# Weight differences fetched, used and stored in another order, and the output projection's transposes in two halves

## The chip, the cores and the metric

The kernel runs on one core of a Trainium2 chip. Its engines work side by side, each through its own queue of instructions in order: TensorE (PE; its weight loads are shown as PEld), VectorE (DVE), ScalarE (ACT), GpSimd (POOL) and SyncE (SP). SP and POOL issue nearly all transfers (DMA). The metric is the device time of one execution in microseconds, as the median of several runs.

## The reference

One layer of a hybrid encoder, for a prompt of 2048 rows (16 tiles of 128) and eight short samples (one more tile, called SAMPLE). All is float32, the model width is 1024.

```python
h   = rms_norm(x, norm_g[0])
z   = h @ w_in                                   # split into heads
att = rms_norm(band_attention(qa, ka, va, rel), g_att)
hb  = mlstm(qb, kb, vb, ib, fb); hb = headnorm(hb) * g_mlstm * sigmoid(ob)
mix = concat([att, hb], axis=-1) @ w_out         # the output projection
x   = x + rms_norm(mix, norm_g[1])
u   = conv3(rms_norm(x, norm_g[2]) @ w_up) + b_conv     # 2 x 2816 columns
x   = x + rms_norm((gelu(u_gate) * u_up) @ w_down, norm_g[3])
```

## The kernel before, in words

A float32 product is made from three products of a rounded form: each operand is split into a high part (a cast on ACT) and a low part (a difference on DVE), and `mm3` (L109 to L113) multiplies high by high, high by low and low by high. So every operand costs ACT one cast and DVE one difference before TensorE can use it: for the weights in `split` (L1352 to L1354), for turned rows in `rows_to_T` (L218 and L219).

The work has three stages. The input projection takes w_in group by group, with the attention and the recurrent memory (mlstm) run beside it in two pipelines. The output projection, `project`, goes over the tiles 0 to 7, SAMPLE, 8 to 15. Then the feed-forward network takes the tiles in three blocks of six, six and five.

The feed-forward products use a scheme of fast matrix multiplication: the operands are cut into 2 x 2 blocks and seven products of sums of blocks stand for eight. For the down-projection the sums of weight blocks are needed: from the blocks B11, B12, B22, B21 of each of the NK = 11 parts of w_down (called 0, 1, 2, 3 in the code), the generator `folds` makes T1 = B12 - B11 (in place of 0), T3 = B22 - B12 (in place of 1), T2 = T1 - B22 (in place of 2) and T4 = B21 + T2 (in place of 3), and stores them in DRAM (`wtd`), from where the down-projection fetches them some hundred microseconds later. A block is 128 x 512, 256 KB. Fetches and stores (`load`, L1210, and `store`, L1217) are issued by POOL; the four operations of a part (`make`, L1213) run on DVE. The three kinds are kept in program order on their engines. The blocks lie in a pool of six buffers, `spare`: a fetch into a buffer waits until the store from it has landed.

`folds` is a generator that is pulled along by `project`: a counter `owed` grows by FOLD_RATE after each half of each sum (68 points in all: 17 tiles, two sums, two halves), and for each whole unit one step of `folds` is traced. What is left at the end is traced after the last tile. So a step is a place in program order; a planner, which works with its own estimate of times, then lays out each engine's queue.

For a tile, `project` does this: the rows `mr` (fetched by SP, two buffers) are normed (ACT square sum L1021, POOL L94 and L100, DVE scale L1023); `turn_rows` transposes them in eight blocks of 128 x 128 on TensorE (L83, into `mT_pt`) and splits them into `mt` (L218, L219); two sums `wo` of 512 columns and 24 products each follow; DVE (L1057) and ACT (L1059) read each sum; POOL makes the factor `n_rs`, DVE adds the residual (L1069), SP stores the row to `x2d` (L1070). The turn of the next tile is traced between the two sums of the present one. The accumulators in PSUM are two of 512 columns (`ps_mm`, tag "mm"), which hold the sums, and two of 1024 columns (`ps_big`, tag "big"), which the attention uses for its scores (`s`) and their transposes (`pt`). Tiles 0 to 7 turn in two halves through `ps_mm`; SAMPLE and tiles 8 to 15 turn in one piece through `ps_big`, with one cast and one difference of 1024 columns.

While tile 7 is worked on the two pipelines are drained, and from tile 8 on the first pieces of the feed-forward input (`h2_units`, transposes `h2T_pt`, through other accumulators) are made beside the projection. After the last tile its weights' memory is given back, the first weights of the up-projection (`wu`, `wuh`, `wul`) are split, and four kept pieces `lated` are fetched and split (`late_B`, L1197 to L1199).

Of the kernel before, what the change touches and what calls it, by code (L numbers as in the profile page):

```python
# [38 lines left out]
HALF = [384, 384, 320]  # L39
PAIRS = [[(((b[j], 0), (b[j + 3], 0)), j * P, P, f"{b[j]}") for j in range(3)] for b in FBLOCKS[:2]]  # L40
NK = NF // 2
FOLD_RATE = 1.0
FAST = (0, 1, 2)
ORDERS = [[f for k in range(NK) for f in (k, k + NK)] if b in FAST else list(range(NF)) for b in range(3)]
B11, B12, B22, B21 = range(4)
# [5 lines left out]
def hymba_step(ctx: ExitStack, tc: tile.TileContext, I: dict, O: dict):  # L51
# [12 lines left out]
    def ps_big(name):  # L64
        return psum.tile([P, 1024], F32, tag="big", name=name)
# [10 lines left out]
    def spare_tile(name):  # L76
        return spare.tile([P, 512], F32, tag="k", name=name)
# [4 lines left out]
    def transpose(out, in_, n=P):  # L82
        nc.tensor.transpose(out, in_, ident[:n, :n])  # L83
# [125 lines left out]
    def rows_to_T(hrow, chunk, j, name, bank):  # L209
        w = 4 if bank is not ps_big else KT  # L210
        for q in range(KT // w):
            pt = bank(f"{name}_pt{q}")
            for k in range(w):
                transpose(pt[:, k * P:(k + 1) * P], hrow[:, (w * q + k) * P:(w * q + k + 1) * P])
            ptv = pt.rearrange("p (k t) -> p k t", k=w)
            hv = chunk[:, 0, w * q:w * q + w, j * P:(j + 1) * P]
            lv = chunk[:, 1, w * q:w * q + w, j * P:(j + 1) * P]
            nc.scalar.copy(hv, ptv)  # L218
            nc.vector.tensor_tensor(lv, ptv, hv, op=ALU.subtract)  # L219
# [733 lines left out]

    wo = []
    g1 = []
    gatt = const.tile([P, 4], F32, name="gatt")

    def w_out_steps():
# [39 lines left out]
    def project(tiles):  # L998
# [25 lines left out]
            s.mt = mt[:, :2 * D].rearrange("p (a k n) -> p a k n", a=2, k=KT)  # L1024

        def turn_rows(s):
            rows_to_T(s.m, s.mt, 0, f"mT{s.t}", ps_mm if s.t < 8 else ps_big)

        fold, owed = folds(), [0.0]
        load(ss[0])  # L1030
        norm(ss[0])
        yield 0.0, 0.3
        turn_rows(ss[0])
        load(ss[1])
        yield 0.9, 1.2
        for n_, s in enumerate(ss):
# [7 lines left out]
            for hf in range(2):  # L1044
                c = slice(hf * 512, hf * 512 + 512)
                acc = ps_mm(f"wo{t}_{hf}")
                for k in range(KT):
                    mm3(acc, s.mt[:, 0, k, :], s.mt[:, 1, k, :], wo[k][0][:, c], wo[k][1][:, c],
                        start=(k == 0), stop=(k == KT - 1))
                    if k % 4 == 3:  # L1050
                        owed[0] += FOLD_RATE
                        while owed[0] >= 1:
                            owed[0] -= 1
                            next(fold, None)
                        yield 2.6, 0.5
                ssq = small.tile([P, 1], F32, tag="wssq", name=f"wssq{t}_{hf}")
                nc.vector.tensor_tensor(m[:, c], acc, g1[0][:, c], op=ALU.mult)  # L1057
                idle = m[:, 512:D] if hf == 0 else s.mt[:, 0, 0:4, :].rearrange("p k n -> p (k n)")
                nc.scalar.activation(idle, acc, AF.Square, accum_out=ssq)  # L1059
                if hf == 0:  # L1060
                    ssa = ssq
                    mean_square(ssa, ssq, D)
                    if nxt:
                        turn_rows(nxt)
                        if n_ + 2 < len(ss):
                            load(ss[n_ + 2])
                        yield 0.9, 1.2
# [133 lines left out]
    def folds():  # L1201

        keep = tc.keep_in_program_order
        sub, plus = ALU.subtract, ALU.add
        live = {}

        def load(k, xs):
            for x in xs:
                live[k, x] = spare_tile(f"fold{k}_{x}")
                keep(nc.gpsimd.dma_start(live[k, x], I["w_down"][k][:, x * 512:(x + 1) * 512]))  # L1210

        def make(k, o, x, y, op):
            keep(nc.vector.tensor_tensor(live[k, o], live[k, x], live[k, y], op=op))  # L1213

        def store(k, xs):
            for x in xs:
                keep(nc.gpsimd.dma_start(wtd[k][:, x * 512:(x + 1) * 512], live.pop((k, x))))  # L1217

        for k in range(NK + 1):
            now, old = k < NK, k > 0  # L1220
            if old:
                make(k - 1, 2, 0, 2, sub)
            if now:
                load(k, (0, 1))
            yield
            if old:
                store(k - 1, (0, 1))
                make(k - 1, 3, 3, 2, plus)
            yield
            if old:  # L1230
                store(k - 1, (2, 3))
            yield
            if not now:
                break
            load(k, (2, 3))
            yield
            make(k, 0, 1, 0, sub)
            yield
            make(k, 1, 2, 1, sub)
            yield  # L1240

    GROUPS = ["va0", "qk0", "qk1", "va1", "qk2", "qk3", "qb0", "vo0", "qb1", "vo1", "qb2", "vo2", "qb3", "vo3"]
# [782 lines left out]
```

## Time and profile before

| | |
|---|---|
| median of 3 runs | 2727.55 us (2724.9 to 2730.89) |
| the profiled execution | 2730.95 us, its span 2729.2 us |
| mean granted TensorE clock | 0.993 |
| busy share of the span: PE, DVE, ACT, POOL | 97%, 68%, 52%, 25% |
| DMA | 555.73 MB, 204 GB/s on average |

A row of a group reads: line, engine, operation, output <- inputs, shape, count, busy time, mean duration in ns, and idle time of the engine before it with what ended it. A row of the timeline reads: start in us from the span's start, duration in us, engine, line, operation, count, and in brackets the idle time before it and its releaser. Matrix products overlap in their rows; two of 512 columns that follow each other start 0.23 us apart.

### The profile page before, as it was taken

Reading aid. Unit: us, or ns where it says so; the run is one execution under the profiler, and the core shown is the slowest. Engines: PE = TensorE matmul, PEld = TensorE weight load, DVE = VectorE, ACT = ScalarE, POOL = GpSimd, SP = SyncE. Lnnn points to the kernel's source line nnn. Section 1 sums busy time; section 2 is a strip of 40 time slices with the busy share of each in tenths; the row PEclk is TensorE's granted clock in tenths of the full one; section 3 lists DMA queues with packets and bytes.
Section 4 is the critical chain, followed back from the end, with each engine's and each line's share of the span. In section 5 each row is a group of like instructions: output and inputs, shape, how many; then the busy total and the mean of one; then the engine's idle time right before and its main releaser. Section 6 shows DMA issues by size and latency. Waiting matters only on the chain. (4 is left out here: it accounts for less than half of the span.)

```text
span 2729.2 us, 47644 instructions
## 1 busy us (share of the span) xinstructions
PE 2651.2 (97%) x16459; PEld 2474.6 (91%) x16459; DVE 1862.9 (68%) x3519; ACT 1421.0 (52%) x2904; POOL 692.4 (25%) x1325
## 2 busy tenths in 40 slices
PE   7999999999999999999999999999999999999998
PEld 7899989998999998777999997899999878999976
DVE  5444555433556666566899997758888876999956
ACT  4345554433556665333555456655455665555554
POOL 1000001201000001354454551023333212556401
PEclk9999999999999999999999999999999999999999
DMA  5545465457644555598787668767886877798875
GB/s 174 156 124 149 125 183 158 151 155 252 194 139 134 152 151 158 178 294 287 281 241 236 204 206 294 237 187 202 228 220 175 256 237 239 213 253 232 259 250 180
DMA packets 333855, 555.73 MB, mean 204 GB/s; under 512 B 61906, under 2 KB 169518, under 8 KB 333294
## 3 DMA queue, kind: packets, MB, share of 16 engines
q1 hardware_dynamic: 250942, 405.06, 48.2%
q0 software_dynamic: 44080, 113.81, 14.5%
q10 hardware_dynamic: 38592, 33.83, 3.7%
q8 instruction: 129, 2.11, 0.3%
q14 instruction: 112, 0.92, 0.1%
HBM read 390.03 MB, written 172.22 MB: 206 GB/s over the span
## 5 line engine op out<-in xcount | busy, mean ns | idle before, releaser
L111 PE MATMUL uec<-B,wuh 128*128 128x384 f32 (+1 forms) x720 | 235.9, 328 | 5.3 <-DVE ug L1524 3.5
L112 PE MATMUL uec<-B,wuh 128*128 128x384 f32 (+1 forms) x720 | 235.1, 327 | 0.0
L113 PE MATMUL uec<-B,wul 128*128 128x384 f32 (+1 forms) x720 | 234.4, 327 | 0.0
L1353 ACT CAST wuh<-wu 128x512 fp32r<-128x512 f32 x255 | 141.7, 618 | 115.9 <-PE uec L112 113.5
L113 PE MATMUL dn<-wdh,al 128*128 128x512 f32 x462 | 186.8, 404 | 3.2 <-DVE al L1354 3.1
L111 PE MATMUL dn<-wdh,ah 128*128 128x512 f32 x462 | 184.3, 399 | 4.7 <-ACT ah L1353 3.3
L1354 DVE TENSOR_TENSOR al<-ar,ah 128x768 fp32r<-128x768 f32 (+2 forms) x141 | 108.5, 779 | 117.2 <-ACT ah L1353 113.9
L112 PE MATMUL dn<-wdl,ah 128*128 128x512 f32 x462 | 183.1, 396 | 0.0
L1353 ACT CAST ah<-ar 128x768 fp32r<-128x768 f32 (+2 forms) x141 | 96.2, 692 | 151.3 <-PE dnm L112 114.4
L1354 DVE TENSOR_TENSOR wul<-wu,wuh 128x512 fp32r<-128x512 f32 x255 | 164.4, 684 | 2.6 <-ACT wuh L1353 2.4
L111 PE MATMUL vo<-wi_h,hT 128*128 128x256 f32 x544 | 156.5, 288 | 1.9 <-ACT vo_st L244 1.8
L113 PE MATMUL vo<-wi_h,hT 128*128 128x256 f32 x544 | 155.2, 285 | 0.0
L112 PE MATMUL vo<-wi_l,hT 128*128 128x256 f32 x544 | 155.0, 285 | 0.0
L1354 DVE TENSOR_TENSOR wdl<-wdr,wdh 128x512 fp32r<-128x512 f32 x231 | 145.4, 685 | 7.6 <-ACT wdh L1353 7.4
L423 ACT ACTIVATE tmp<-tmp,mn 128x640 f32<-128x640 f32 (+4 forms) x128 | 97.7, 763 | 89.1 <-DVE mn L422 78.0
L111 PEld LDWEIGHTS uec<-B,wuh 128*128 128x128 f32 x720 | 135.1, 188 | 8.1 <-issue 3.5
L422 DVE CUSTOM_DVE_ANT_0 tmp<-s,nb 128x640 f32<-128x640 f32 (+4 forms) x128 | 94.1, 737 | 64.3 <-PE s L412 63.9
L112 PEld LDWEIGHTS uec<-B,wuh 128*128 128x128 f32 x720 | 135.2, 188 | 0.2
L113 PEld LDWEIGHTS uec<-B,wul 128*128 128x128 f32 x720 | 135.1, 188 | 0.0
L1353 ACT CAST wdh<-wdr 128x512 fp32r<-128x512 f32 x231 | 127.4, 620 | 13.2 <-PE uec L112 7.6
L435 DVE TENSOR_TENSOR ptl<-pt,pth 128x640 fp32r<-128x640 f32 (+4 forms) x128 | 93.8, 738 | 58.4 <-ACT pth L434 57.5
L111 PE MATMUL qk<-hT,wi_h 128*128 128x384 f32 (+1 forms) x384 | 128.2, 334 | 0.6 <-ACT gates L293 0.5
(473 smaller groups left out, 8968.6 us busy)
## 6 DMA issues: line engine op xcount, KB each, us to landing
wu<-in_w_up SPq DMA_DIRECT2D x220, 256.0 KB, 5.1
wu<-wsd SPq DMA_DIRECT2D x176, 256.0 KB, 4.9
wdr<-wtd SPq DMA_DIRECT2D x132, 256.0 KB, 5.8
wi_raw<-in_w_in SPq DMA_DIRECT2D x52, 512.0 KB, 4.2
wdr<-in_w_down SPq DMA_DIRECT2D x99, 256.0 KB, 4.6
wsd<-ws POOLq DMA_DIRECT2D x88, 256.0 KB, 4.9
ar<-ad_S SPq DMA_DIRECT2D x50, 384.0 KB, 3.9
kraw<-kTd SPq DMA_DIRECT2D x112, 128.0 KB, 3.3
```

The lines of the kernel that those rows point to most:

```text
L111: nc.tensor.matmul(out, ah, bh, start=start, stop=False, skip_group_check=onto)
L112: nc.tensor.matmul(out, ah, bl, start=False, stop=False, skip_group_check=onto)
L113: nc.tensor.matmul(out, al, bh, start=False, stop=stop, skip_group_check=onto)
L422: nc.vector.tensor_tensor_reduce(o_, s_, b_, 1.0, 3e38, ALU.add, ALU.min, accum_out=mn)
L423: nc.scalar.activation(tmp[:, :n], tmp[:, :n], AF.Exp, bias=mn, scale=-1.0, accum_out=rsum[:, i % 4, hh:hh + 1])
L435: nc.vector.tensor_tensor(s.ptl[:, sl, qc], ptv, s.pth[:, sl, qc], op=ALU.subtract)
L1353: nc.scalar.copy(h, r)
L1354: nc.vector.tensor_tensor(l, r, h, op=ALU.subtract)
```

## The change

Two things. First, `turn_rows`: tiles 0 to 3 turn through `ps_mm` as before; all later ones (4 to 7, SAMPLE, 8 to 15) turn in two halves through `ps_big`, of which each half uses the first 512 columns. `rows_to_T` works in halves for any accumulator that is not `ps_big` itself, so the new function gives two tiles, two casts and two differences for each turn.

Second, `folds`: the same four differences in another order. Before, a part took six steps: fetch 0 and 1; (the last part's stores 0 and 1); (stores 2 and 3); fetch 2 and 3; T1; T3. T2 and T4 of a part fell into the first two steps of the next part's loop. Now it is: fetch 1 and 0; -; -; fetch 2; fetch 3; T1; and T3, T2 and T4 fall into the first three steps of the next part, with one store per step. FOLD_RATE goes from 1.0 to 1.1, and the loop after the last part runs through its empty steps.

```diff
-FOLD_RATE = 1.0
+FOLD_RATE = 1.1
...
+    TURN_BIG = 4
...
         def turn_rows(s):
-            rows_to_T(s.m, s.mt, 0, f"mT{s.t}", ps_mm if s.t < 8 else ps_big)
+            rows_to_T(s.m, s.mt, 0, f"mT{s.t}", ps_mm if s.t < TURN_BIG else lambda name: ps_big(name)[:, 0:512])
...
         for k in range(NK + 1):
             now, old = k < NK, k > 0
             if old:
-                make(k - 1, 2, 0, 2, sub)
+                make(k - 1, 1, 2, 1, sub)
             if now:
-                load(k, (0, 1))
+                load(k, (1, 0))
             yield
             if old:
-                store(k - 1, (0, 1))
+                store(k - 1, (1,))
+                make(k - 1, 2, 0, 2, sub)
+            yield
+            if old:
+                store(k - 1, (0,))
                 make(k - 1, 3, 3, 2, plus)
             yield
             if old:
-                store(k - 1, (2, 3))
+                store(k - 1, (2,))
+            if now:
+                load(k, (2,))
             yield
-            if not now:
-                break
-            load(k, (2, 3))
+            if old:
+                store(k - 1, (3,))
+            if now:
+                load(k, (3,))
             yield
-            make(k, 0, 1, 0, sub)
-            yield
-            make(k, 1, 2, 1, sub)
+            if now:
+                make(k, 0, 1, 0, sub)
             yield
```

## The prediction

> **What bounds the kernel now.** I read the page first, then the windows of the stage that the diff touches, then who TensorE waited for in it.
>
> ```profile
> PE 2651.2 (97%) x16459; PEld 2474.6 (91%) x16459; DVE 1862.9 (68%) x3519; ACT 1421.0 (52%) x2904; POOL 692.4 (25%) x1325
> L113 PE MATMUL wo<-wo,mt x272: 388/396/794, 1050.8 to 1306.1; 128*128 128x512 f32 x136
> ```
>
> TensorE is busy for 97% of the span, so only its pauses are to be had. The output projection, where both edits lie, runs from 1050.8 to 1306.1 us. The windows (length, then busy time of PE, PEld, DVE, ACT, POOL, granted clock, DMA share, GB/s) from tile 4 on:
>
> ```profile
> 1110.00:1178.00 68.00, 64.41 (x314) 51.84 (x314) 35.91 (x79) 22.69 (x69) 29.20 (x57) 1.00 0.67 208
> 1178.00:1200.00 22.00, 17.78 (x75) 13.41 (x73) 11.42 (x23) 4.76 (x12) 11.48 (x21) 0.84 0.95 311
> 1200.00:1306.00 106.00, 103.04 (x486) 82.97 (x486) 69.22 (x92) 42.52 (x90) 52.71 (x99) 0.98 0.90 303
> 1306.00:1330.00 24.00, 21.27 (x110) 20.29 (x109) 22.69 (x32) 14.18 (x21) 9.35 (x12) 0.93 0.84 321
> ```
>
> The worst stretch is 1178 to 1200: TensorE busy for 17.78 of 22 us, at a clock of 0.84. TensorE's waits from 1110 to 1310 (total, times, longest):
>
> ```profile
> PE wo L113 <- DVE mt L219: 3.5, 2, 2.6
> PE wo L111 <- ACT mt L218: 3.2, 3, 1.6
> PE mT_pt L83 <- ACT mx L1059: 1.4, 2, 0.7
> ...
> PE wo L111 <- DVE mt L219: 0.5, 2, 0.3
> PE wo L111 <- ACT mt L1059: 0.4, 1, 0.4
> ```
>
> These five, 9.0 us, all hang on turning the rows of a tile (transposes, ACT cast L218, DVE difference L219). Behind two of the pauses the clock halves:
>
> ```profile
> 1183.60:1190.50 6.90, 5.36 (x13) 4.20 (x14) 4.84 (x11) 0.00 (x0) 5.70 (x11) 0.51 0.97 382
> 1252.00:1255.30 3.30, 1.62 (x9) 0.88 (x6) 1.59 (x2) 2.21 (x5) 0.79 (x2) 1.00 0.98 377
> 1255.30:1258.80 3.50, 3.50 (x8) 2.78 (x9) 1.49 (x2) 1.10 (x2) 2.96 (x5) 0.51 1.03 414
> ```
>
> Half a clock over 6.9 and 3.5 us costs 3.4 and 1.7 us more.
>
> **Part 1: tiles 4 to 7 turn in the big accumulators.** The two halves of their rows now lie in the pair of accumulators that the projection itself needs: the second half waits until the first sum is read (L1059), and the second sum until the first half is cast. These are the rows of 1.4 and 0.5 us: 1.9 us. Upper bound, by twice that for pauses that the modelled ends hide: 3.8. I take 1.9, the measured rows. The cover is that nobody else wants the big pair then: the attention's scores and their transposes used it last at
>
> ```profile
> L411 PE MATMUL s<-kh,qs x224: 221/309/497, 88.9 to 1062.5; 128*128 128x320 f32 x96, 128*128 128x128 f32 x8, 128*128 128x384 f32 x8
> L83 PE MATMUL pt<-ident,tmp x560: 270/272/330, 100.7 to 1070.5; 128*128 128x128 f32 x187
> ```
>
> and tile 4 turns after 1110. Without that cover a turn would wait for one evacuation of the attention, by the nearest rows (a cast and a difference of 512 columns, the fence below: 0.586 + 0.687) an estimate of 1.3 us or more, 5 us over four tiles.
>
> **Part 2: from the sample tile on, two halves in place of one whole.**
>
> ```profile
> L218 ACT CAST mt<-mT_pt 128x512 fp32r<-128x512 f32 x16 | 9.4, 586 | 4.4 <-PE mT_pt L83 4.4
> L218 ACT CAST mt<-mT_pt 128x1024 fp32r<-128x1024 f32 x9 | 9.1, 1011 | 12.7 <-PE mT_pt L83 12.7
> L219 DVE TENSOR_TENSOR mt<-mT_pt,mt 128x1024 fp32r<-128x1024 f32 x9 | 11.0, 1221 | 12.4 <-ACT mt L218 12.4
> L219 DVE TENSOR_TENSOR mt<-mT_pt,mt 128x512 fp32r<-128x512 f32 x16 | 11.0, 687 | 2.5 <-ACT mt L218 2.5
> ```
>
> Nine tiles get one ACT and one DVE instruction more: 2 x 0.586 - 1.011 = 0.16 us on ACT and 2 x 0.687 - 1.221 = 0.15 us on DVE each, 1.4 us per engine in all. From 1200 to 1306 ACT is busy for 42.52 and DVE for 69.22 of 106 us, which hides it; uncovered it is 2.8 us. In return the first product can start after a cast of 0.586 us rather than 1.011: 0.4 us wherever TensorE stands on the cast. Three places after the sample tile (tiles 8, 12 and 15 by the order of the waits): 1.2 us. The half clock after 1255.3 follows a window in which TensorE was busy for 1.62 of 3.30 us; with 0.4 to 0.8 us less pause that is near the edge, so I count half of its 1.7 us: 0.8. Together 2.0, bounds 0 and 5.0: the five rows' 9.0 us less the 1.9 of part 1 and the sample tile's 1.16 + 2.61 leave 3.3 us of such waits, and the clock is 1.7.
>
> **Part 3: the order of the differences.** Nothing is added: 44 fetches and 44 stores on POOL's queue, 256 KB each, and 44 differences on DVE, before and after.
>
> ```profile
> L1213 DVE TENSOR_TENSOR fold<-fold,fold 128x512 f32<-128x512 f32 x44 | 30.2, 687 | 13.1 <-DMA fold<-in_w_down 10.3 <-issue 2.4
> DVE fold L1213 <- DMA fold<-in_w_down: 10.3, 6, 3.0
> ```
>
> They cost DVE 30.2 us of work and 12.7 us of standing before them. The sample tile's pause comes from one such stand (PE, POOL, DVE in order of time):
>
> ```profile
> 1179.03 1.04 PE L83 MATMUL mT_pt<-ident,mr 128*128 128x128 f32 x8
> 1181.22 0.50 PE L111 MATMUL wo<-wo,mt 128*128 128x512 f32 x1 [1.16 <-ACT mt L218]
> 1185.14 0.79 PE L113 MATMUL wo<-wo,mt 128*128 128x512 f32 x1 [2.61 <-DVE mt L219]
> ```
> ```profile
> 1177.26 1.69 POOL L1210 DMA_DIRECT2D fold<-in_w_down  x3
> ```
> ```profile
> 1183.19 0.69 DVE L1213 TENSOR_TENSOR fold<-fold,fold 128x512 f32<-128x512 f32 x1 [2.40 <-issue]
> 1183.80 0.15 DVE L667 SCALAR_TENSOR_TENSOR ad<-num 128x2 f32<-128x2 f32 x1
> 1183.87 1.22 DVE L219 TENSOR_TENSOR mt<-mT_pt,mt 128x1024 fp32r<-128x1024 f32 x1
> ```
>
> DVE stood for 2.40 us at a fold difference. The row names no releaser; I read it as a block fetched from 1177.26 on that landed near 1183, because the same line waits for its fetches elsewhere (below). L219 was queued behind it, and TensorE behind L219. In the old order a loop of six steps fetches two blocks at step 1 and two at step 4, and takes the differences at 5, 6, 1 and 2; the tightest is the one at 6, two steps after its fetch. In the new one the blocks come at 1, 1, 4 and 5 and are used at 6, 1, 2 and 3; the tightest has three steps. A step is one of 68 points in 255 us, 3.75 us, and at the rate of 1.1 it is 3.4 us: the least room grows from 7.5 to 10.2 us. Landing (least, median, most) between 1240 and 1315:
>
> ```profile
> DMA to landing us min/median/max: 4.3/6.5/9.0
> ```
>
> So 7.5 us did not cover 9.0, and 10.2 does, if the planner keeps to the steps: three fetches in a bunch at 1177.26 show that it crowds them, so the room is a mean. I take 2.4 us for the fetch and 0.4 for the half cast, out of 1.16 + 2.61, and the 3.4 us of clock: 6.2. Bounds: 0.4, if DVE finds another late operand there, and 7.2.
>
> At the end of the stage:
>
> ```profile
> 1304.65 2.26 DVE L1213 TENSOR_TENSOR fold<-fold,fold 128x512 f32<-128x512 f32 x3 [3.02 <-DMA fold<-in_w_down]
> 1307.43 0.68 DVE L1354 TENSOR_TENSOR wul<-wu,wuh 128x512 fp32r<-128x512 f32 x1
> ```
> ```profile
> 1308.16 0.44 PE L113 MATMUL ua<-B,wul 128*128 128x384 f32 x1 [0.60 <-DVE wul L1354]
> 1318.58 0.44 PE L112 MATMUL ua<-B,wuh 128*128 128x384 f32 x1 [1.96 <-DVE B L1199]
> 1320.10:1323.60 3.50, 3.50 (x13) 3.50 (x12) 3.43 (x3) 0.00 (x0) 0.00 (x0) 0.52 1.02 402
> ```
>
> DVE waits 3.02 us for the last fetches, spends 2.26 us on the last differences, and only then reaches the first weights of the up-projection. At 1.1 steps per point the last difference is step 69 of 72, at point 63: some five points, 19 us, before the end. What is late there: 0.60 + 1.96 + 1.7 of clock = 4.3 us. DVE stays nearly full (22.69 of 24 us), and the split rows of the first block still have to be fetched after the projection has let go of its memory; so I take half, 2.1, bounds 0 and 4.3.
>
> The step has a price on POOL. A fetch waits there until the store of the block that held its buffer has landed; in the old order two of four blocks come back after two steps and two after four, in the new one three after two and one after three, and two steps shrink to 6.8 us. Already now (the stage's waits, then POOL in order of time):
>
> ```profile
> POOL fold L1210 <- DMA wtd<-fold: 9.6, 6, 3.9
> ```
> ```profile
> 1253.73 0.54 POOL L1210 DMA_DIRECT2D fold<-in_w_down  x1 [3.38 <-DMA wtd<-fold]
> 1258.01 0.55 POOL L100 TENSOR_TENSOR att_rs<-att_ms,nhalf 128x1 f32<-128x1 f32 x1
> ```
> ```profile
> 1258.60 0.49 DVE L1023 TENSOR_SCALAR mr<-mr,att_rs 128x512 f32<-128x512 f32 x1 [0.72 <-POOL att_rs L100]
> 1262.33 1.04 PE L83 MATMUL mT_pt<-ident,mr 128*128 128x128 f32 x8
> ```
>
> Behind the waiting fetch stand the norm's POOL operations, then L1023, then the transposes. The rows were ready at 1259.1 and used at 1262.3: 3.2 us of slack hid the wait of 3.38. I charge 1 us for what outgrows it and 1 us for a fold traffic 10% denser where the DMA share is already 0.90 to 0.95; bounds 0 and the slower rival's 20.
>
> **Sum:** 1.9 + 2.0 + 6.2 + 2.1 - 2.0 = 10.2 us. The profiled execution took 2730.95 us (span 2729.2) and would take 2720.7. It lay 3.4 us above the median of the runs, 2727.55; the forecast for that median is 2717.3.
>
> **A rule against it.** The Trainium skill (TensorE: Matmul & The Clock Gate, section "Why this matters for your kernels") has it that only pauses over some 3 us, one whole idle window, bring the clock down. Then pauses of 1.16 and 2.61 us would not have cost 3.4 us; the rows above disagree, since a window with 1.62 of 3.30 us busy was followed by 0.51.
>
> **Rivals.**
> A, the forecast, own range 2712 to 2722: 50%.
> B, every pause of the turns goes, with its clock: 9.0 + 3.4 + 1.7 + 4.3 = 18.4, 2709. For it: three steps cover the longest landing. Against: turns placed behind the last product of their tile (sample tile, 12) still wait for a cast. 10%.
> C, the stall moves: with the fold traffic 10% denser on DMA engines 0.90 to 0.95 busy, landings pass 10.2 us and DVE stands at differences again. Left are 1.9 + 1.2 - 1 = 2.1: 2725.5. Against: the median landing is 6.5. 20%.
> D, the waits go but the clock halves all the same, its windows being set off by something else: 10.2 - 3.4 - 0.8 - 0.9 = 5.1, 2722.4. 8%.
> E, slower: POOL's waits for returned buffers pass the 3.2 us of slack. Two waits of 9.0 - 6.8 = 2.2 us ahead of one norm are 4.4 us; TensorE loses 1.2 us and 1.7 of clock, 2.9 per tile. Five of the nine late tiles eat the gain of 12.2; at seven it is 20 - 12 = +8, 2735.5. 12%.
>
> **How the numbers follow.** Under 0.2% (5.5 us) a measurement of this kernel can't be told from no change. Faster: A and B, 60%; same: C and D, 28%; slower: E, 12%. The range 2708 to 2732 holds A, C, D and most of B, and leaves out most of E.
>
> **What would show it.** Part 1: no wait of mT_pt for L1059 between tiles 4 and 7. Part 2: 34 casts L218 of 512 columns, none of 1024. Part 3: DVE's wait for fetches (now 10 us) near zero, the last difference before 1290, clock 1.00 from 1180 to 1260. The forecast would be wrong if POOL waits over 15 us for the stores (9.6 now), if L1023 appears among TensorE's releasers with more than 2 us, or if the planner puts more turns behind the last product of their tile, so that the cast's waits grow past 3.2 us.

## The result, and the profile after

The changed kernel takes 2746.47 us (median of 6 runs, 2745.34 to 2751.11), the kernel before 2728.74 us beside it (6 runs, 2724.9 to 2735.08). The ratio is 1.006, with a 95% interval of 1.0047 to 1.0072: slower by some 17 us, where 10 us of gain were forecast. In the lines below, those behind line 957 have a number one higher than before (L1213 is now L1214), and those behind the loop of `folds` a number seven higher (L1354 is now L1361).

The whole loss lies in the stage that the diff touches. The projection's products of the changed kernel:

```profile
L113 PE MATMUL wo<-wo,mt x272: 388/396/632, 1051.1 to 1322.7; 128*128 128x512 f32 x136
```

They end at 1322.7, 16.6 us later than the 1306.1 of before, from nearly the same start (1051.1 against 1050.8). TensorE's waits in that stage, from 1050 on (total, times, longest):

```profile
PE h2T_pt L1141 <- DVE x2r L1133: 9.9, 2, 8.8
PE wo L113 <- DVE mt L219: 6.3, 4, 2.5
PE mT_pt L83 <- ACT mx L1060: 4.4, 2, 3.9
PE ms L728 <- DVE w L722: 3.8, 1, 3.8
PE wo L111 <- ACT wo L984: 1.0, 1, 1.0
PE wo L111 <- ACT mt L218: 0.8, 1, 0.8
PE h2T_pt L1141 <- DVE t L1167: 0.7, 1, 0.7
PE mT_pt L83 <- PE wo L113: 0.4, 1, 0.4
PE wo L111 <- DVE mt L219: 0.3, 1, 0.3
PE mT_pt L83 <- DVE mr L1024: 0.2, 1, 0.2
```

They sum to 27.8 us. All such rows of the kernel before, over its whole stage, sum to 14.2 us; the prediction's five rows hold 9.0 of them, and the largest part of the rest is 2.2 us, ahead of 1110, of this row:

```profile
PE mT_pt L83 <- ACT mx L1059: 3.6, 4, 1.8
```

The waits of L111 for casts, which part 2 went for, fell from 3.2 to 0.8 us, and no turn of tiles 4 to 7 waits for L1060 any more. What came in their place is large: 8.8 us ahead of the first feed-forward transposes (h2T), 3.8 us ahead of a product of the recurrent memory (L728), 3.9 us ahead of the turn of an early tile, and 6.3 us in all ahead of products that wait for the low part of the turned rows. The windows from 1110 on in which the granted clock was down (columns as in the prediction), and the one ahead of the last of them in time:

```profile
1267.40:1270.80 3.40, 0.90 (x5) 0.57 (x4) 2.01 (x4) 0.09 (x1) 1.02 (x3) 1.00 0.88 244
1270.90:1274.30 3.40, 3.40 (x9) 2.63 (x8) 2.91 (x4) 1.23 (x4) 2.54 (x3) 0.51 1.04 345
1223.10:1236.80 13.70, 5.86 (x22) 4.69 (x23) 7.15 (x8) 10.06 (x22) 9.73 (x15) 0.50 0.54 212
1151.50:1158.30 6.80, 5.55 (x16) 4.72 (x17) 5.00 (x10) 2.47 (x8) 3.32 (x6) 0.50 0.30 77
```

Half of TensorE's busy time in the three at 0.50 is lost: (3.40 + 5.86 + 5.55) / 2 = 7.4 us. The same sum over the two windows of before (5.36 and 3.50) is 4.4. (One more window of 3.4 us, near 1086, is in both kernels.) So 13.6 us of waits and 3.0 of clock make up the 16.6.

The pause near 1085 comes first. VectorE before, then VectorE and TensorE in the changed kernel:

```profile
1081.69 0.23 DVE L521 TENSOR_SCALAR hgm<-hgm 128x128 f32<-128x128 f32 x1 [1.61 <-DMA hgm<-in_g_mlstm]
```
```profile
1083.89 0.23 DVE L521 TENSOR_SCALAR hgm<-hgm 128x128 f32<-128x128 f32 x1 [4.01 <-DMA hgm<-in_g_mlstm]
```
```profile
1085.49 0.66 PE L83 MATMUL mT_pt<-ident,mr 128*128 128x128 f32 x4 [3.94 <-ACT mx L1060]
```

L521 scales a row of gains (hgm) that SP fetches at 1077.21 before and at 1077.27 now. Behind it in VectorE's queue stands the reading of a finished sum (L1058), behind that ACT's (L1060), and the turn waits for the accumulator: 3.94 us, against 1.80 before. In the changed kernel POOL issues the fetch of a block (part 0, block 3) at 1078.20, just behind SP's fetch; before, that block's fetch went out at 1064.64.

Who else stood, from 1085 to 1330:

```profile
POOL fold L1211 <- DMA wtd<-fold: 27.6, 12, 6.3
POOL wtd L1218 <- DVE fold L1214: 27.2, 11, 7.5
DVE fold L1214 <- DMA fold<-in_w_down: 24.4, 9, 4.1
ACT B L1129 <- DMA x2r<-x2d: 21.0, 5, 12.4
```

The prediction had the first at 9.6 and the third at 10.3 us before, and expected the third near zero. The pause of 3.8 us, at L728, shows how these rows hang together. VectorE's queue, then POOL's, in order of time:

```profile
1144.52 0.28 DVE L733 TENSOR_TENSOR num<-num,ms 128x129 f32<-128x129 f32 x1
1148.45 0.69 DVE L1214 TENSOR_TENSOR fold<-fold,fold 128x512 f32<-128x512 f32 x1 [3.65 <-DMA fold<-in_w_down]
...
1152.41 0.28 DVE L722 TENSOR_TENSOR w<-ms,w 128x128 f32<-128x128 f32 x1
```
```profile
1134.11 0.62 POOL L1218 DMA_DIRECT2D wtd<-fold  x1 [4.22 <-DVE fold L1214]
...
1135.27 0.54 POOL L1218 DMA_DIRECT2D wtd<-fold  x1
...
1142.86 0.62 POOL L1211 DMA_DIRECT2D fold<-in_w_down  x1 [3.09 <-DMA wtd<-fold]
```

POOL stood 4.22 us at a store for its difference. The fetches behind it in the queue went out late, the last of them after 3.09 us more for the landing of a store, at 1142.86. VectorE came to the difference that wants this block at 1144.8 and stood for 3.65 us; L722 stood behind it (with 1.39 us more for a factor that POOL makes), and TensorE's product behind L722 began at 1152.75, after 3.8 us. A late difference holds a store, the store holds the next fetches, and these make the next difference late: that would be a ring (the experiments call this the ring theory).

At this place the ring is not closed. The difference that the store waited for (part 0, block 2, at 1133.12) was late only by its place in VectorE's queue: its blocks had been fetched 69 us before. And the kernel before has the same difference with the same room of 2.0 us. There VectorE stood for 2.02 us (until 1139.96), and no wait of TensorE over 0.7 us followed; what differs is that the fetch took 4.0 us to its use, against 5.6, and what stood behind in the queue. A turn that is closed stands near the end of the stage. VectorE had stood for 3.68 us at a difference of part 7, until 1255.99. Then POOL, VectorE and TensorE:

```profile
1258.20 0.55 POOL L1218 DMA_DIRECT2D wtd<-fold  x1 [3.87 <-DVE fold L1214]
...
1263.74 1.26 POOL L1211 DMA_DIRECT2D fold<-in_w_down  x2
```
```profile
1268.79 0.69 DVE L1214 TENSOR_TENSOR fold<-fold,fold 128x512 f32<-128x512 f32 x1 [2.65 <-DMA fold<-in_w_down]
```
```profile
1270.14 0.50 PE L113 MATMUL wo<-wo,mt 128*128 128x512 f32 x1 [2.50 <-DVE mt L219]
```

The store waited 3.87 us for part 7's next difference, and the fetch of a block of part 8 (1263.74) stands behind it, with a fetch, two more stores and the norm's operations between. VectorE stood for 2.65 us at the difference that wants this block, and TensorE for 2.50 us behind that; the last window of half clock follows.

The room between a fetch and its use can be taken from the two traces for all 44 differences: the time at which VectorE was done with what stands ahead of a difference, less the time at which POOL issued the latest of the blocks that it wants. The queues as built tell which belong together.

| room, issue to VectorE's arrival | least | median | under 6 us |
|---|---|---|---|
| before | 2.0 us | 10.0 us | 10 of 44 |
| changed | 0.7 us | 7.2 us | 16 of 44 |

It shrank where it was meant to grow. The queues as built suggest why. POOL's queue for parts 6 and 7 (L a fetch, S a store, part and block) and the first differences in VectorE's:

```
POOL, before   L6.2 L6.3 L7.0 L7.1  S6.0 S6.1 S6.2 S6.3  L7.2 L7.3 L8.0 L8.1  S7.0 S7.1 S7.2 S7.3
POOL, changed  L7.1 S6.0 L7.0 S6.1 S6.2 L7.2 S6.3 L7.3 L8.1 S7.0 S7.2 L8.0 S7.1 S7.3
DVE, before    0.0 0.1 0.2 0.3 2.0 1.0 1.1 1.2 1.3 2.1 2.2 2.3 3.0
DVE, changed   0.0 0.1 0.2 0.3 2.0 1.0 1.1 1.2 2.1 2.2 1.3 2.3 3.0
```

Before, fetches and stores go in bunches of four; now single stores, each of which waits for its difference, stand between the fetches. And in both kernels the planner put the first difference of part 2 ahead of all of part 1: the one at 1148.45 is this one, its block fetched 2 us ahead, while part 1's had been fetched from 1122.91 on. This alone does not set the two kernels apart.

The large pause, of 8.8 us, has another chain. SP, then ACT, VectorE and TensorE:

```profile
1201.34 0.42 SPq L1071 DMA_DIRECT2D x2d<-mx  x1
...
1210.92 0.33 SPq L1044 DMA_DIRECT2D mx<-in_x_prompt  x1
1211.31 0.42 SPq L1090 DMA_DIRECT2D g<-in_norm_g  x1
1211.78 1.48 SPq L1113 DMA_DIRECT2D x2r<-x2d  x2
1213.36 0.50 SPq L1017 DMA_DIRECT2D mr<-mixd  x1
1213.90 0.97 SPq L1113 DMA_DIRECT2D x2r<-x2d  x2
```
```profile
1223.49 1.06 ACT L1129 ACTIVATE B<-x2r 128x1024 fp32r<-128x1024 f32 x1 [12.44 <-DMA x2r<-x2d]
```
```profile
1228.22 1.28 DVE L1133 SCALAR_TENSOR_TENSOR x2r<-x2r,n_rs,g 128x1024 f32<-128x1024 f32 x1 [11.20 <-ACT mx L1060]
```
```profile
1229.56 1.12 PE L1141 MATMUL h2T_pt<-ident,x2r 128*128 128x128 f32 x4 [8.79 <-DVE x2r L1133]
```

SP's fetch of mx writes a buffer whose rows are stored to x2d from 1201.34, and goes out at 1210.92. Behind it stand both pairs of x2r, so seven transfers of 512 KB are issued within 4 us. ACT reaches the square of the first pair (L1129) and stands for 12.44 us with the projection's own evacuation (L1060) behind it. VectorE's row names L1060, which ended at the same time; by the built queues L1133 waits for the square and for the norm's factor n_rs, which POOL makes from it at 1227.63, in 0.56 us. In the kernel before the first x2r pair stands one tile earlier in SP's queue, ahead of that mx fetch, and the two pairs went out 16 us apart.

### The profile page after: what moved, and what is told of

The parts are those of the page before. It is cut to its first block, busy times and chain, and to the rows that moved or that the text cites. A ratio compares the mean times of both kernels' runs of the same rounds, so it can differ in the third digit from the quotient of the medians.

```text
span 2744.9 us, 47646 instructions
## 1 busy us (share of the span) xinstructions
PE 2657.1 (97%) x16459; PEld 2480.6 (90%) x16459; DVE 1862.3 (68%) x3528; ACT 1422.0 (52%) x2913; POOL 690.3 (25%) x1325
## 5 line engine op out<-in xcount | busy, mean ns | idle before, releaser
L111 PE MATMUL uec<-B,wuh 128*128 128x384 f32 (+1 forms) x720 | 236.0, 328 | 5.7 <-DVE ug L1531 4.2
L111 PE MATMUL dn<-wdh,ah 128*128 128x512 f32 x462 | 183.6, 397 | 3.9 <-ACT ah L1360 2.2
L1361 DVE TENSOR_TENSOR al<-ar,ah 128x768 fp32r<-128x768 f32 (+2 forms) x141 | 108.5, 779 | 115.1 <-ACT ah L1360 114.8
L1361 DVE TENSOR_TENSOR wul<-wu,wuh 128x512 fp32r<-128x512 f32 x255 | 164.2, 683 | 7.0 <-DMA x2d<-mx 4.6
L111 PE MATMUL vo<-wi_h,hT 128*128 128x256 f32 x544 | 157.2, 289 | 1.9 <-ACT vo_st L244 1.8
L1361 DVE TENSOR_TENSOR wdl<-wdr,wdh 128x512 fp32r<-128x512 f32 x231 | 145.4, 685 | 8.0 <-ACT wdh L1360 5.9
L111 PEld LDWEIGHTS uec<-B,wuh 128*128 128x128 f32 x720 | 135.1, 188 | 8.8 <-issue 4.2
L111 PE MATMUL qk<-hT,wi_h 128*128 128x384 f32 (+1 forms) x384 | 129.1, 336 | 0.6 <-ACT gates L293 0.5
```

Of the source, the lines that this page charges most:

```text
L111: nc.tensor.matmul(out, ah, bh, start=start, stop=False, skip_group_check=onto)
L1361: nc.vector.tensor_tensor(l, r, h, op=ALU.subtract)
```

## The experiments

"Stage" is the time from the first to the last product of the projection in the profile of the run: 256.2 us before, 272.5 changed. Starts of the stage differ by up to 10 us between profiles (1043 to 1053), so stages are compared by length and kernels by their medians. A stage is that of one execution, which can lie some us from its kernel's median (e4's 6.7 us above it, e14's 6.3 above, e6's 7.5 below).

### Each part alone

```diff
e1_rate          FOLD_RATE = 1.1
e2_order         the new body of the loop in folds
e3_turns         the new turn_rows
e4_fold          e1_rate and e2_order together
e11_turn4_whole  ps_mm if s.t < 4 else ps_big
```

> The kernel before with the rate of the difference steps alone at 1.1. Fold theory (the differences' fetches and stores make DVE and POOL stand, and this reaches TensorE): part of the 17.7 us, some 2735, with DVE's wait for fetches above the 10.3 us of before. Turns theory (the halves through the big accumulators shift the planner's order): 2728, no change. Planner theory (any small edit redraws the order of the queues by as much): anywhere from 2718 to 2745, without relation to the waits of the differences.

> The kernel before with the new order of fetches, uses and stores alone, at the old rate of 1.0 and with the old turns. Fold theory: some 2738, POOL's wait for returned buffers above 20 us (9.6 before, 27.6 in the changed kernel). Turns theory: 2728. Planner theory: anywhere from 2718 to 2745.

> The kernel before with the turns in two halves through the big accumulators from tile 4 on, and the old differences. Fold theory: 2723 to 2726, the gain of the parts 1 and 2 of the prediction (3.9 us) without its loss. Turns theory: 2740 to 2746. Planner theory: anywhere from 2718 to 2745.

> The kernel before with the new order and the rate of 1.1, and the old turns: all of the change but the turns. Fold theory: 2746 to 2750, the whole loss. Turns theory: 2728. Planner theory: anywhere from 2718 to 2745, and not the sum of the order's and the rate's own effects.

> The kernel before with the turns of tiles 4 to 7 whole in the big accumulators, and nothing else: no halves, old order, old rate. The prediction's first part: 1.9 us gained, 2725 to 2727 us; the rest of the new turns' 7 us would then be the halves' work. If the early turns are the whole of it: 2719 to 2722 us.

| edit on the kernel before | median us | ratio, 95% interval | stage us |
|---|---|---|---|
| e1: rate | 2723.04 | 0.9984, 0.9970 to 0.9999 | 257.2 |
| e2: order | 2729.18 | 1.0012, 0.9998 to 1.0025 | 261.7 |
| e4: order and rate | 2729.93 | 1.0015, 0.9999 to 1.0030 | 267.5 |
| e3: turns | 2720.80 | 0.9977, 0.9965 to 0.9989 | 250.2 |
| e11: turns of tiles 4 to 7 whole, no halves | 2726.91 | 1.0001, 0.9988 to 1.0015 | 255.6 |

No part alone loses what the change loses. The turns gain 0.23%; as tiles 4 to 7 alone give nothing that shows, most of it is the halves' work. The new order gives nothing, and VectorE's wait for fetches does not fall in it: 14.6 us with the order, 18.2 with order and rate, against 10.3. Were the parts independent, all three would give 0.9977 x 1.0015 = 0.999. Of the expectations the fold theory failed in e1, e2 and e4, and e3 came out below its range; the planner theory, with 2718 to 2745 for each, could hardly fail.

One loss does belong to the order alone, the stand at hgm (L521). In all ten runs with the new order (the changed kernel, e2, e4, e5, e7, e9, e13, e15, e16, e17) POOL issues a block 0.9 us behind SP's fetch of hgm, and VectorE stands for 3.0 to 4.8 us; in the ten with the old order no block goes out there, and it stands for 1.2 to 1.6 us, but 2.9 in e11. So some 2 us of the 16.6 come from the place of one fetch, with the differences or without them (e13). That the block's transfer delays hgm's is the likely reason; no run moves that fetch alone.

### Two parts together

```diff
e6_turns_rate    the new turn_rows and FOLD_RATE = 1.1, old order
e7_turns_order   the changed kernel with FOLD_RATE = 1.0
```

> The kernel before with the new turns and the rate of 1.1, in the old order of the differences. Sum of the single effects (turns -5.3 us, rate -3.0 us against the runs of before): 2718. Interaction theory (turns and any denser differences meet at the pause near tile 9): 2735 or more.

> The changed kernel at the old rate of 1.0: new turns and new order. Sum of the single effects (turns -5.3, order +3.1): 2724. Interaction theory: 2738 to 2746, that is the order and the turns together lose what neither loses alone, and the rate adds little.

e6 took 2743.11 us (1.0055, 1.0030 to 1.0080), e7 2737.52 us (1.0037, 1.0024 to 1.0051). So either half of the fold edit turns the gain of the new turns into a loss. The places differ: TensorE waits in e6 for 6.1 us at h2T and 7.1 at products whose accumulator L1060 has yet to read, in e7 not at h2T but for 5.9 us at such products, 3.4 at the product of the recurrent memory and 2.9 at each of two turns. POOL's wait for returned buffers is 29.6 us in e6 and 8.7 in e7, and it was 16.9 in e1, which is not slower than before: its size alone does not decide.

### The late x2r rows

```diff
e5_after_x2r, e8_turns_x2r (the changed kernel; the new turns alone)
-        pipes[:] = [Pipe(h2_units(0, lead=6)), Pipe(iter([]))]
+        pipes[:] = [Pipe(h2_units(0, lead=3)), Pipe(iter([]))]
...
-            if not late:
+            for _ in range(3 if late else 1):
                 yield 0.0, 0.0

e9_x2r_queue, e10_turns_queue, e12_before_queue
(the changed kernel; the new turns alone; the kernel before), all this and
-                    fetch = nc.sync.dma_start(rows_[t], x2d[t])
+                    fetch = (nc.scalar if late else nc.sync).dma_start(rows_[t], x2d[t])
```

> The changed kernel with one edit: the rows that the feed-forward input is made of (x2r) are fetched three steps of their pipeline earlier, and used at the same step as now. Fetch theory (the loss is the one pause at 1220 to 1240, where ACT stands for 12.4 us at the square sum of rows that have not landed, ahead of the projection's own evacuations): 2727 to 2732, at least 14 us under the changed kernel, ACT's wait at L1129 below 4 us. Fold theory (POOL's and DVE's waits for the differences' transfers set the stage's length): 2740 to 2746, no change.

> The kernel before with the new turns, the old differences and the earlier fetch of x2r. Fetch theory: the turns alone still lose 3.6 us and two stretches of half clock to ACT's wait at these rows; without it 2713 to 2717, 4 to 8 us under the turns alone. Fold theory: 2720, as the turns alone.

> The changed kernel, but the x2r rows of the first feed-forward block are fetched from ACT's queue instead of SP's and asked for three pipeline steps earlier, so that they no longer stand behind SP's mx fetch (which waits for the store of the tile before) and the two pairs no longer start within 3 us of each other. Fetch theory (the pause of 8.8 us ahead of the first h2T transposes and the half clock of 13.7 us behind it come from four x2r fetches that land together and late): ACT's wait for x2r falls from 12.4 us to below 4 us, the h2T wait below 3 us, and the time from 2746.5 to about 2731 us, level with the kernel before. Density theory (PE waits for DVE and POOL wherever folds, turns and x2r meet, and the x2r fetch is only where it showed this time): the h2T wait goes and other waits of PE grow by about as much; 2740 us or more.

> The kernel before with the new turns alone, and the x2r rows fetched from ACT's queue as in the run beside it. Fetch theory: the stretch between the turns of tiles 9 and 10, 22 us with the new turns alone against 13.8 us before, shrinks to 14 to 16 us; the time falls from 2720.8 to 2712 to 2716 us. Density theory: no gain, 2719 to 2723 us.

> The kernel before with the x2r rows fetched from ACT's queue and three steps earlier, and nothing else: what that move does by itself. In this kernel the two pairs were 16 us apart already and ACT waited at most 3.1 us for them. Fetch theory: no change, 2726 to 2729 us. If the move by itself shifts the planner's order: a change of 4 us or more either way.

| kernel | median us | ratio, 95% interval | stage us |
|---|---|---|---|
| e5: changed, asked for earlier | 2738.65 | 1.0047, 1.0031 to 1.0064 | 270.7 |
| e8: turns, asked for earlier | 2720.73 | 0.9981, 0.9969 to 0.9993 | 254.2 |
| e9: changed, ACT's queue | 2737.89 | 1.0048, 1.0032 to 1.0064 | 260.9 |
| e10: turns, ACT's queue | 2721.66 | 0.9977, 0.9965 to 0.9990 | 247.9 |
| e12: before, ACT's queue | 2727.48 | 1.0006, 0.9993 to 1.0020 | 256.6 |

e5 was no test of the pause: in SP's queue the x2r fetches still stood behind the mx fetch and went out at 1204.4, with the stage's start at 1044.0 no earlier in the stage than before the edit (160.4 us into it, against 161.7), and h2T still waited 8.5 us. In e9 the fetch did move. Its waits, ACT's and TensorE's:

```profile
ACT B L1129 <- DMA x2r<-x2d: 6.4, 4, 2.6
```
```profile
PE h2T_pt L1141 <- DVE x2r L1133: 1.6, 2, 1.1
PE wo L113 <- DVE mt L219: 7.1, 3, 4.7
```

The pause at h2T is gone, and the stage is 11.6 us shorter. But the kernel is still 10.8 us slower than the one before, against 17.7, and the intervals of the two ratios overlap; 2731 us were expected if the fetch were all. A new pause of 4.7 us has come, and behind it stands VectorE again:

```profile
1225.78 0.68 DVE L1167 TENSOR_TENSOR t<-h2T_pt,b 128x512 f32<-128x512 f32 x1
1230.90 0.69 DVE L1214 TENSOR_TENSOR fold<-fold,fold 128x512 f32<-128x512 f32 x1 [4.43 <-DMA fold<-in_w_down]
1231.51 0.68 DVE L219 TENSOR_TENSOR mt<-mT_pt,mt 128x512 fp32r<-128x512 f32 x1
```

With the turns alone (e8, e10) and in the kernel before (e12) the move changes nothing. The bunch of x2r fetches is there with the turns alone too (1190.9 to 1193.3 in e3) and costs nothing at h2T there (0.2 us). So the fetch is one place where the loss shows, not the whole of it. The time lies between the ranges of both theories (about 2731, or 2740 and more).

### The differences out of VectorE's queue

```diff
e13_nodiff (the changed kernel), e14_before_nodiff (the kernel before)
         def make(k, o, x, y, op):
-            keep(nc.vector.tensor_tensor(live[k, o], live[k, x], live[k, y], op=op))
+            return
```

> The changed kernel with the 44 differences left out: every fetch and store of the blocks stays at its step, but what is stored is what was fetched, so the down-weights are not combined and VectorE never stands for a fold's fetch. Ring theory (a difference that waits for its fetch holds VectorE's queue, with turns, evacuations and decays behind it; POOL's store then waits for the difference, and the next fetches stand behind that store): PE's waits for VectorE of 3.8 us (the decay, 1152.75), 2.5, 1.9 and 1.4 us (products) go, as does most of the 8.8 us at h2T; the stage of 272.5 us falls to 245 to 252 us and the time to 2720 to 2727 us. Transfer theory (the same bytes by the same queues make x2r and mx late whatever VectorE does): the h2T pause stays at 6 us or more, the time at 2735 us or more.

> The kernel before with the 44 differences left out in the same way: the floor that the run beside it is read against. Ring theory: VectorE's 10.3 us of waits go, but few of them stood ahead of PE (the largest are 2.6 and 1.6 us), so 4 to 9 us fall away: 2718 to 2723 us; the changed kernel without differences is then level or up to 5 us faster than this, by its turns. Transfer theory: the changed kernel without differences stays 10 us or more above this one.

Without the differences the blocks are stored as they were fetched. e13 took 2716.16 us (0.9957, 0.9944 to 0.9970) and e14 2718.79 us (0.9964, 0.9951 to 0.9977), with stages of 248.9 and 248.3 us. Without the differences the changed kernel becomes faster by 1.03% (1.0060 - 0.9957), some 28 us, and the kernel before by 0.36%, some 10; the changed one is no longer the slower, by the medians it is 2.6 us faster. In the changed kernel without differences:

```profile
POOL fold L1211 <- DMA wtd<-fold: 30.2, 14, 5.6
DVE mx L1070 <- POOL n_rs L100: 27.8, 14, 5.0
ACT B L1129 <- DMA x2r<-x2d: 14.2, 6, 6.4
```

POOL waits for returned buffers no less than with the differences (27.6), and the norm's results reach VectorE later (27.8, against 15.0); TensorE's waits on that road are 1.7 us (the transposes behind L1024). The bytes are the same. So transfers and POOL's waits by themselves are not the loss. The run has a limit: with the differences gone, the planner also put the first x2r pair one tile earlier in SP's queue, where the kernel before has it, so e13 takes away the second chain of the changed kernel too.

### Fetches ahead of stores

```diff
e15_load_first (the changed kernel), e16_queue_load_first (e9_x2r_queue); the same for block 3
-            if old:
-                store(k - 1, (2,))
             if now:
                 load(k, (2,))
+            if old:
+                store(k - 1, (2,))
```

> The changed kernel with two lines exchanged in two steps of the new order: the fetches of blocks 2 and 3 are issued ahead of the stores of the same step, not behind them, so that a store that waits for its difference no longer holds the next fetch back. Same work, same buffers. Ring theory: VectorE's wait for fetches falls from 24.4 to 10 to 16 us, POOL's for returned buffers stays; time 2733 to 2741 us. Transfer theory: no change, 2744 to 2749 us.

> Both repairs on the changed kernel: the exchanged lines, and x2r fetched from ACT's queue three steps earlier. Ring theory: the two add up, 2725 to 2732 us, level with the kernel before. If the exchanged lines do nothing: 2736 to 2740 us, as with the moved x2r fetch alone.

e15: 2743.09 us (1.0048, 1.0024 to 1.0073), stage 268.4. POOL's wait for differences fell from 27.2 to 10.9, but VectorE's for fetches only from 24.4 to 19.3 us (from 29.7 to 26.5 with the stands at a difference for which the row names something else), less than expected; the interval of the ratio takes in the changed kernel's, so the run decides nothing on the time. e16: 2752.08 us (1.0094, 1.0070 to 1.0117), a miss for both expectations. Its stage is 266.0 us and VectorE waits 27.6 us for fetches; some 15 us of its loss lie behind the stage (1438.3 us from the last product to the end, against 1423.1 before), the largest wait there being 4.5 us at the first weights' difference (L1361), against 0.6 before. Two edits that each left the time alone or helped it did harm together, as the parts of the change did.

### The differences on POOL

```diff
e17_pool_diff (the changed kernel), e18_turns_pool (the new turns alone)
-            keep(nc.vector.tensor_tensor(live[k, o], live[k, x], live[k, y], op=op))
+            keep(nc.gpsimd.tensor_tensor(live[k, o], live[k, x], live[k, y], op=op))
```

> The changed kernel with the 44 differences computed on POOL, in the queue that also issues their fetches and stores; the same results, and nothing of the folds left in VectorE's queue. Ring theory (the place in VectorE's queue costs the time): a difference that waits for its fetch holds only POOL, behind which stand the norms' small operations, whose lateness cost little where the differences were left out (VectorE waited 27.8 us for n_rs there, in 2716.2 us); POOL gets 44 operations of an estimated 0.7 to 1.5 us each (estimate from 0.47 us for 128x256 there and 0.69 us for 128x512 on VectorE). Time 2716 to 2728 us. If the differences cost through what they do to stores and fetches wherever they are computed: 2740 us or more.

> The kernel before with the new turns, old order and old rate, and the differences on POOL. Ring theory: VectorE's 14.9 us of waits for fetches and the 3.65 us of PE behind one of them go; 2713 to 2719 us, below both kernels and below the new turns alone (2720.8 us). If POOL's longer queue makes n_rs, the stores of x2d and so x2r late: 2722 us or more.

e17: 2751.78 us (1.0087, 1.0074 to 1.0100), e18: 2739.48 us (1.0042, 1.0026 to 1.0057); both are slower than with the differences on VectorE, and the ring theory's forecasts, 2716 to 2728 us for e17 and 2713 to 2719 for e18, failed. In e17's profile:

```profile
L1214 POOL TENSOR_TENSOR fold<-fold,fold 128x512 f32<-128x512 f32 x43 | 59.0, 1372 | 15.1 <-DMA fold<-in_w_down 14.0
```
```profile
L1024 DVE TENSOR_SCALAR mr<-mr,att_rs 128x512 f32<-128x512 f32 x16 | 14.1, 883 | 3.8 <-POOL att_rs L100 3.8
```
```profile
PE ua L113 <- DVE wul L1361: 12.2, 1, 12.2
PE mT_pt L83 <- ACT mx L1060: 4.7, 2, 4.2
```

Two things are to be kept apart. In the stage e17 is 12.3 us shorter than the changed kernel (260.2 us), and h2T waits for x2r no longer than 0.6 us in all. But e18's stage is 260.2 us too, 10.0 longer than that of the turns alone: on POOL the differences cost time in the stage as well, and there the order and the rate make no difference to its length. Nor does e17 show that the large pause needs a VectorE that stands. Its x2r fetches stand behind an mx fetch as in the changed kernel, but they went out earlier, 151.1 us into the stage against 161.6, and their rows were there after 7.9 us, not 11.7. And e18 has such a pause with no difference in VectorE's queue:

```profile
ACT B L1129 <- DMA x2r<-x2d: 21.9, 4, 12.6
```
```profile
1207.09 0.80 PE L111 MATMUL wo<-wo,mt 128*128 128x512 f32 x1 [5.59 <-ACT mx L1060]
```

ACT stood for 12.6 us at the square of x2r, and TensorE for 5.59 us at a product whose accumulator the evacuation behind it had yet to read. So late x2r rows are enough for a pause of this kind.

Behind the stage e17 takes 1441.1 us, 18.9 more than the changed kernel; 12.2 of them are the wait above: the first weights' difference (L1361) now stands behind four differences of the first feed-forward block in VectorE's queue, which wait for their casts on ACT. A difference takes 1372 ns on POOL, at the dear end of the estimate, and VectorE's L1024 took 883 ns instead of 488.

## Why the prediction was wrong

**The parts on the turns were right.** Part 1: no turn of tiles 4 to 7 waits for L1060. Alone (e11) it changed the median by less than its interval of about 3.7 us, so its 1.9 us are neither confirmed nor refuted. Part 2: all 34 casts of the stage have 512 columns, and the wait for casts fell from 3.2 to 0.8 us. The two together (e3) gained some 5 to 6 us by medians and ratio (2720.80 against 2726.08), where 3.9 were forecast.

**The step that failed is the room in part 3:** "the least room grows from 7.5 to 10.2 us. [...] So 7.5 us did not cover 9.0, and 10.2 does". Steps were taken for time. A fetch goes out when POOL reaches it, and a difference is wanted when VectorE reaches it: the room measured was 2.0 us at the least before and 0.7 after, its median fell from 10.0 to 7.2, and VectorE's wait rose from 10.3 to 24.4 us instead of falling near zero. At 1142.86 a fetch that program order has five steps ahead of its use went out 2 us ahead of it, because POOL had stood 4.22 us for a difference and 3.09 us for a store, and because the planner had drawn the difference forward. The forecast saw the doubt ("if the planner keeps to the steps") and did not price it. Part 3 was to gain 6.2 + 2.1 - 2.0 = 6.3 us; alone (e4) it gained nothing (1.0015, 0.9999 to 1.0030). The second step that failed is the sum itself, which took the parts to be independent: e6 and e7 show that they are not, and most of the loss is in that. The sample tile's pause did go: that tile's wait is 0.78 us at 1196.77 and the clock was up there. Its 3.4 us of clock were half of the 6.9 us window, though; TensorE was busy for 5.36 of them, so 2.7 were to be had. Of the two waits at the transition the one of 1.96 us is gone, but the one of 0.60 for the first weights' difference is 1.6 us now, and the last difference begins at 1312.5, not before 1290.

**The price on POOL** had the right quantity and the wrong road. POOL's wait went from 9.6 to 27.6 us, past the 15 that were named as the sign of a wrong forecast. But it was led through the norm's results and L1024 to the transposes, as in rival E, and that road cost 0.2 us (TensorE's row of mT_pt and L1024); e13 bears 30.2 us of such waits with 1.7 us on that road. As far as the traces show it, the price is paid where VectorE stands at the difference, with turns, sums and the recurrent memory's weights (L722) behind it.

**The rivals.** C named that place ("DVE stands at differences again") but not the cause: it laid it to dense DMA engines. The median time of the blocks' fetches from issue to landing is 5.7 us over the stage, against 5.8 before: they did not grow longer. At the pause of 1152.75 the fetch took 5.6 us to its use (1142.86 to 1148.45). E named the cause (returned buffers) but not the place, and came nearest in time, 2735.5. Neither had SP's queue in it: that with the new turns both pairs of x2r stand behind an mx fetch, and that ACT's evacuation stands behind the square of x2r; nor the fetch of hgm beside a block's. The change was costed part by part against waits of the kernel before.

**The clock.** The prediction held that pauses under 3 us bring it down, against the rule of the Trainium skill (TensorE: Matmul & The Clock Gate, section "Why this matters for your kernels"). The changed kernel agrees with the prediction: the window with 0.90 of 3.40 us busy, whose longest wait was 2.50 us, was followed by 0.51.

**What stays open.** That the loss needs the differences is shown by e13 and e14, with a limit: e13 moved x2r in SP's queue too. That the ring of late differences, stores and fetches starts it is read from the traces and not shown; e15, which should have loosened it, left the room as it was (median 7.4 us, 15 of 44 under 6) and decides nothing. Neither the room nor VectorE's stands order the runs. The new turns alone, which gain, have a median room of 8.7 us with 13 of 44 under 6, and e7, slower by 0.37%, has 9.4 us with 7 of 44. VectorE's stands at differences, whatever the row names, are 18.3 us in e6, slower by 0.55%, and 18.6 in e4, which is level. So a rival stands: each edit has the planner lay the queues of ACT, VectorE and SP out anew, and how much the new layout costs is not told by the differences alone. Why the new turns bear either fold edit so badly, when each alone is harmless, is not settled. A seventh buffer for the blocks, which would take away POOL's wait alone, was not tried. No variant with the differences in it beat the new turns alone, at 0.9977 of the kernel before (e8 and e10, the same with x2r asked for earlier, and from ACT's queue, are their equals).

## What to carry to other kernels

Room counted in steps of a generator is worth only as much as the queue that issues the fetch: before it is turned into us, follow that queue and count what it waits for between the two steps. When an operation off the critical path (here a weight difference) sits in the in-order queue of an engine that the critical path uses, its operands must be there when it is reached, since everything behind it stands too. And edits that each move a planner's queues need not add up: measure them in pairs before you sum them.

## What the hardware showed that was not expected

POOL's difference of 128x512 took 1372 ns, against 686 on VectorE, and while POOL did 43 of them VectorE's L1024, with the same work, went from 488 to 883 ns on average: in this kernel, work moved from VectorE to POOL slowed VectorE's own. It comes in two sizes: ten of the sixteen L1024 took 0.48 to 0.49 us and six 1.51 to 1.66, and five of these six lie on a difference on POOL for 1.2 to 1.3 us, while of the ten only one does, for 0.3. L219, of which one operand lies in an accumulator in PSUM, took 685 ns on average, against 684. The Trainium skill (GPSIMD Engine Reference, section "Specifications") has the two engines share their interfaces to SBUF, with contention for some VectorE instructions; the rows are in keeping with that, and give its size here. From within the pause of 8.8 us on, the granted clock was at 0.50 for 13.7 us, in which TensorE was busy for 5.86; with the waits of 2.50 and 3.8 us it was so for 3.4 and 6.8 us.
